# RG-LRU gates by block: features reordered, stacked remainders, tanh gates and two output phases

## The chip, the cores and the metric

One core of one Trainium2 chip runs the whole program in one launch. The metric is device time in microseconds: the median of three runs was 1885.63 us (1885.54 to 1885.96). All rows below come from one profiled execution of 1887.7 us, whose span from first to last instruction is 1885.9 us.

## The reference

Two layers of a diffusion transformer act on 256 latent tokens (x) and 256 context tokens, model width 1024. Each layer is a half-weighted SwiGLU FFN, a mixer, and a second FFN, each behind an RMS norm with shift and scale from a conditioning vector. The mixer of layer 0 is an RG-LRU of width 1280, that of layer 1 a retention. All arithmetic is float32. The part that matters here:

```python
def block_diag(x, w, b):                     # 8 blocks of 160 features
    xg = x.reshape(bsz, t, LRU_BLOCKS, LRU_BLK)
    return (jnp.einsum('btgi,gij->btgj', xg, w) + b).reshape(bsz, t, D_RNN)

def lru_coeffs(xc, gate_w, gate_b, lam):     # for each of two directions
    r = jax.nn.sigmoid(block_diag(xf, gate_w[0], gate_b[0]))
    ig = jax.nn.sigmoid(block_diag(xf, gate_w[1], gate_b[1]))
    log_a = -LRU_C * r * jax.nn.softplus(-lam)
    a = jnp.exp(log_a)
    b = jnp.sqrt(-jnp.expm1(2.0 * log_a)) * (ig * xf)
...
    # h = a*h + b forward and backward over the tokens, the context first;
    # xc is a 4-tap convolution over tokens of h @ w_x
    gate = jax.nn.gelu((h @ w_g))
    return (hsum * gate) @ w_out
```

## The kernel before

Activations lie features on partitions, tokens (256 context, then 256 latent) along the free dimension. A weight is a 128x128 tile; eight of them are one 512 KB transfer. Every product of two float32 numbers is done as three TensorE products of rounded parts (`mm3`, L140 to L144): high x high, high x low, low x high. The high part of a weight tile is a ScalarE copy (L112), the low part a VectorE subtraction (L138). `w(key)` (L117) hands out the next weight: it fetches and splits two tiles ahead (LA = 2), emits the low parts in the second half of a tile, and calls `pump` (L160), which takes one step each from two background lists, `bgv` (steps that begin on VectorE) and `bga` (ScalarE). So the order of work on each engine is the order in which the Python code emits it; engines run in order and wait for each other by semaphores. PSUM has eight banks of 512 columns, handed out in a ring.

`lru` (L534) works on ten chunks of 128 features. `first_group` computes four chunks of projections in two halves of tokens. Then, for chunk j: one projection for the Gelu gate, `gates(j)` (L596), the gates' evaluation `coeffs(j)` on ScalarE (Sigmoid four times, Exp twice, Tanh twice, Sqrt), a projection for a convolution (`conv`, L566), and the vector steps of the chunk before (L646), with the scans. A block of 160 features lies across chunks of 128, so `gates(j)` multiplies two or three row chunks for each column chunk (L37), 26 pairs in all, most of a tile being zeros. The output projection comes in three phases: chunks 0 and 1 before j = 6, chunks 2 to 5 behind the loop, and 6 to 9 in `boundary` (L404), which works in two halves of 256 tokens, sums squares for the next norm (`sq_acc`, `stat`), and begins the next FFN's inputs (`h_chunk`). `out_proj` (L359) adds each product to x on VectorE (L393).

In the two places where only the latent tokens go on (behind the retention, and at the end), `boundary` sums squares over eight chunks on VectorE, sums over partitions by a product with ones (L296), takes the inverse root on VectorE (L305 to L316), and keeps TensorE running with ten products of zeros (`warm`, L319) before `bcast` spreads the result.

## Time and profile before

| | |
|---|---|
| median of three runs | 1885.63 us |
| profiled execution | 1887.7 us, span 1885.9 us |
| TensorE busy | 1857.2 us (98%) |
| VectorE busy | 1283.8 us (68%) |
| ScalarE busy | 718.2 us (38%) |
| GpSimd busy | 0.2 us |
| mean granted TensorE clock | 0.991 of 2.4 GHz |

PE is TensorE, PEld its weight loads, DVE VectorE, ACT ScalarE. A busy share over the span is a mean over stages with different limits; the stretches tell more. A matmul's duration includes its way through the array, so the time one costs is the distance to the next one's start.

### The profile page before, as it was taken

To read this page: it belongs to the slowest core of one execution; us is meant where nothing else is said; L and a number is where in the kernel's file an instruction comes from. 1 tells how busy PE (TensorE), PEld (TensorE's weight loads), DVE (VectorE), ACT (ScalarE), POOL (GpSimd) and SP (SyncE) were. 2 spreads that over 40 slices of the span, in tenths; PEclk is the share of its full clock that TensorE was granted. 3 is DMA by queue.
4 is the path that set the end of the run, shared out by engine and by line. 5 is a ranking of instruction groups with operands and counts; after the bars stand their busy time and mean duration, and the time that the engine had idled before them with its cause. 6 is when DMAs were issued, how large, how long until landed. Compare 5 with 4: busy or idle time off the path is not lost.

```text
span 1885.9 us, 25731 instructions
## 1 busy us (share of the span) xinstructions
PE 1857.2 (98%) x10278; PEld 1621.5 (86%) x10278; DVE 1283.8 (68%) x2110; ACT 718.2 (38%) x984; POOL 0.2 (0%) x4
## 2 busy tenths in 40 slices
PE   8999999999999899999999999999999999999998
PEld 7888888897888888888889888888898899989997
DVE  7877697676899975767577655455576465675555
ACT  3322222248989342222224322222244243344442
POOL 0000000000000000000000000000000000000000
PEclk8999999999999999999999999999999999999999
DMA  8355454422322244454452445444324333355552
GB/s 319 127 211 187 167 189 181 145 90 79 100 90 90 79 157 168 158 185 172 143 172 94 154 150 187 145 171 178 102 80 150 124 123 118 97 160 182 176 186 101
DMA packets 77736, 277.52 MB, mean 147 GB/s; under 512 B 8752, under 2 KB 10032, under 8 KB 77616
## 3 DMA queue, kind: packets, MB, share of 16 engines
q1 hardware_dynamic: 77616, 275.88, 42.5%
q8 instruction: 80, 1.31, 0.3%
q14 instruction: 40, 0.33, 0.1%
HBM read 274.80 MB, written 1.05 MB: 146 GB/s over the span
## 4 chain that ended last, share of the span: by engine, by line
PE 92%; DVE 5%; ACT 1%; issue 1%; DMA 0%; SPq 0%; ACTq 0%; DVEq 0%
PE ps L142 30%; PE ps L144 30%; PE ps L143 30%; PE ps L237 1%; DVE x L393 1%; DVE wlo L138 1%; DVE hlo L138 1%; DVE h L354 0%; ACT h L348 0%; DVE acc L286 0%; PE ps L323 0%; PE ps L329 0%; PE ps L296 0%; DVE ht L346 0%; DMA x<-xt 0%
## 5 line engine op out<-in xcount | busy, mean ns | idle before, releaser
L142 PE MATMUL ps<-h,whi 128*128 128x512 f32 (+1 forms) x1824 | 641.1, 352 | 0.0
L144 PE MATMUL ps<-h,wlo 128*128 128x512 f32 (+1 forms) x1824 | 639.7, 351 | 1.2 <-DVE wlo L138 1.2
L143 PE MATMUL ps<-h,whi 128*128 128x512 f32 (+1 forms) x1824 | 640.3, 351 | 0.5 <-DVE h L354 0.5
L138 DVE TENSOR_TENSOR wlo<-wraw,whi 128x1024 fp32r<-128x1024 f32 x349 | 417.7, 1220 | 78.3 <-ACT whi L112 78.2
L112 ACT ACTIVATE whi<-wraw 128x1024 fp32r<-128x1024 f32 x349 | 357.3, 1050 | 275.8 <-PE ps L143 225.6
L144 PEld LDWEIGHTS ps<-h,wlo 128*128 128x128 f32 x1824 | 345.8, 190 | 47.7 <-DVE wlo L138 1.9
L143 PEld LDWEIGHTS ps<-h,whi 128*128 128x128 f32 x1824 | 345.9, 190 | 46.5 <-DVE h L354 1.6
L142 PEld LDWEIGHTS ps<-h,whi 128*128 128x128 f32 x1824 | 345.9, 190 | 44.9 <-ACT whi L112 0.3
L242 DVE SCALAR_TENSOR_TENSOR junk<-modraw,cB 128x1024 bf16<-128x1024 f32 x240 | 293.1, 1221 | 4.6
L393 DVE SCALAR_TENSOR_TENSOR x<-ps,M,x 128x256 f32<-128x256 f32 x296 | 132.5, 479 | 160.7 <-PE ps L144 160.3
L157 ACT ACTIVATE A<-sil 128x512 fp32r<-128x512 f32 (+1 forms) x88 | 50.9, 579 | 474.0 <-DVE sil L486 474.0
L142 PE MATMUL ps<-A,whi 128*128 128x512 f32 (+1 forms) x608 | 217.9, 358 | 0.0
L143 PE MATMUL ps<-A,whi 128*128 128x512 f32 (+1 forms) x608 | 217.9, 358 | 0.0
L144 PE MATMUL ps<-A,wlo 128*128 128x512 f32 (+1 forms) x608 | 217.9, 358 | 0.0
L486 DVE TENSOR_TENSOR sil<-ps,sil 128x512 f32<-128x512 f32 (+1 forms) x88 | 54.8, 623 | 159.8 <-PE ps L144 151.9
L144 PEld LDWEIGHTS ps<-A,wlo 128*128 128x128 f32 x608 | 114.9, 189 | 16.9
L143 PEld LDWEIGHTS ps<-A,whi 128*128 128x128 f32 x608 | 114.9, 189 | 16.9
L142 PEld LDWEIGHTS ps<-A,whi 128*128 128x128 f32 x608 | 114.9, 189 | 16.7
L158 DVE TENSOR_TENSOR A<-sil,A 128x512 fp32r<-128x512 f32 (+1 forms) x88 | 55.1, 626 | 56.7 <-ACT A L157 56.7
L485 ACT ACTIVATE sil<-ps 128x512 f32<-128x512 f32 (+1 forms) x88 | 47.3, 538 | 80.4 <-PE ps L144 79.9
L348 ACT ACTIVATE h<-ht,M 128x256 fp32r<-128x256 f32 x88 | 42.4, 504 | 91.5 <-DVE ht L346 91.5
L142 PE MATMUL ps<-A,hhi 128*128 128x256 f32 x192 | 54.8, 285 | 0.0
(171 smaller groups left out, 2065.3 us busy)
## 6 DMA issues: line engine op xcount, KB each, us to landing
wraw<-w SPq DMA_DIRECT2D x371, 512.0 KB, 4.3
modraw<-modw SPq DMA_DIRECT2D x144, 512.0 KB, 4.3
x<-xt SPq DMA_DIRECT2D x8, 256.0 KB, 4.9
mask<-mask SPq DMA_DIRECT2D x4, 512.0 KB, 6.0
out<-fin SPq DMA_DIRECT2D x8, 128.0 KB, 1.8
cs<-rope SPq DMA_DIRECT2D x1, 256.0 KB, 2.6
vecs<-vecs SPq DMA_DIRECT2D x1, 251.0 KB, 7.4
ident<-ident SPq DMA_DIRECT2D x1, 64.0 KB, 2.0
```

Source lines behind the costliest of these rows:

```text
L112: nc.scalar.activation(hi, raw, AF.Copy)
L138: self.nc.vector.tensor_tensor(lo, raw, hi.bitcast(F32), ALU.subtract)
L142: mm(ps, whi, xhi, start=first, stop=False, skip_group_check=True)
L143: mm(ps, whi, xlo, start=False, stop=False, skip_group_check=True)
L144: mm(ps, wlo, xhi, start=False, stop=last, skip_group_check=True)
L157: self.nc.scalar.activation(hi, src, AF.Copy)
L158: self.nc.vector.tensor_tensor(lo, src, hi.bitcast(F32), ALU.subtract)
L242: nc.vector.scalar_tensor_tensor(self.junk, raw, 1.0, self.cB[:, c, :], op0=ALU.mult, op1=ALU.mult, accum_out=M[:, idx, k, c:c + 1])
L348: nc.scalar.activation(h[:, 0, a:b], tt, AF.Identity, bias=M[:, 3 * n, k, c:c + 1])
L393: nc.vector.scalar_tensor_tensor(self.x[d][:, a0:a1], ps[:, a0 - c0:a1 - c0], M[:, gidx, d, c:c + 1], self.x[d][:, a0:a1], op0=ALU.mult, o ...
L485: nc.scalar.activation(s[:, :w], pa[:, c0:c1], AF.Silu)
L486: nc.vector.tensor_tensor(s[:, :w], pg[:, c0:c1], s[:, :w], ALU.mult)
```

## The change

The 1280 features are put in another order: first the leading 128 features of each block of 160 (chunks 0 to 7), then the eight remainders of 32, four to a chunk (chunks 8 and 9). A block's gate needs five column groups: four gates of 128 columns, and one group that holds the four gates' remainders of 32 columns each. The rows of the block are its 128 features, by `mm3`, and its 32 remainder features, whose three products are stacked along the contraction: `S` holds high, low and high parts of the remainder on partitions 0 to 95 (three copies by DMAs that GpSimd issues), and the weight tile holds the remainder rows three times, of which rows 64 to 95 are turned into the low part. So a block takes 5 x 3 + 5 products of 512 columns. Chunk 8's vector steps run with block 3, chunk 9's with block 7.

The sigmoids become tanh of half the argument, 1 + tanh is folded into scales and vector steps; `1 - r` moves from VectorE to ScalarE; the convolution reads its taps from PSUM without a copy to `cbuf`. Two buffers R instead of three. The output comes in two phases: chunks 0, 1, 2, 3, 8 before block 6, and the rest at the end, where chunks 4, 5, 6 are summed over all 512 tokens into eight banks (`out_sum`) and chunks 7 and 9 are added in `boundary`. Where only latent tokens go on, the last chunk's squares go to the partition sum as a second operand instead of an addition, and nine warm products follow instead of ten. There are 368 weight transfers instead of 371.

```diff
+LRU_PERM = np.concatenate([np.arange(160 * b, 160 * b + P) for b in range(8)]
+                          + [np.arange(160 * b + P, 160 * b + 160) for b in range(8)])
+LRU_ORDER = (0, 1, 2, 3, 8, 4, 5, 6, 7, 9)
...
     def w_low(self):
-            self.nc.vector.tensor_tensor(lo, raw, hi.bitcast(F32), ALU.subtract)
...
+                if kinds[o]:
+                    sub(hi[64:96, c], raw[64:96, c], hi[64:96, c].bitcast(F32), ALU.subtract)
+                else:
+                    sub(lo[:, c], raw[:, c], hi[:, c].bitcast(F32), ALU.subtract)
...
     def sq_acc(self, st, d, c0, c1):
+            if d == KD - 1 and st.get("two"):
+                st["last"] = s
+                return
...
+    def out_sum(self, acts, key):
+
+        banks = [self.psum() for _ in range(KD)]
+        for i, act in enumerate(acts):
+            for d in range(KD):
+                self.mm3(banks[d], *self.w(key(i, d)), *act(0, 2 * T), i == 0, False)
+        return banks
...
-            y = self.stat(st[0]["acc"], 2, 1.0 / D)
-            self.warm(10)
+            y = self.stat([st[0]["acc"], st[0]["last"]], 2, 1.0 / D)
+            self.warm(9)
...
-        banks = self.first_group([wx(0), wx(1), wg(0), wg(1)], False, hooks)
+        banks = self.first_group([wx(8), wx(0), wx(1), wg(0)], False, hooks)
...
             def first():
-                nc.scalar.activation(buf[:, :, 1:T + 1], p3, AF.Copy)
-                nc.scalar.activation(x, ps, AF.Identity, bias=cb[:, j:j + 1], scale=cw[:, j, 1:2])
+                act(x, ps, AF.Identity, bias=cb[:, j:j + 1], scale=cw[:, j, 1:2])
                 tap(0)
...
+        def stack_x(b):
+
+            t = S[b] = pool.tile([P, 512], F32R, tag="S", name="S", bufs=2)
+            src = xs[8 + b // 4]
+            q = slice(32 * (b % 4), 32 * (b % 4) + 32)
+            for i, part in enumerate((0, 1, 0)):
+                nc.gpsimd.dma_start(t[32 * i:32 * i + 32], src[q, part])
...
+        def gates(b):
+
+            out = [self.psum() for _ in range(5)]
+            for g in range(5):
+                self.mm3(out[g], *self.w(("lg", b, g)), xs[b][:, 0], xs[b][:, 1], True, False)
+            for g in range(5):
+                w, _ = self.w(("ls", b, g))
+                nc.tensor.matmul(out[g], w[0:96], S[b][0:96], start=False, stop=True, skip_group_check=True)
+            if b % 4 < 2:
+                stack_x(b + 2)
             return out
...
+        def gate(b, g, ps):
+
+            t = (R, I)[g % 2][b]
+            act(t[:, g // 2], ps[g], AF.Tanh, bias=gb[:, b, g:g + 1], scale=0.5)
+
+        def gate_rem(b, g, ps):
+            t = (R, I)[g % 2][8 + b // 4]
+            q = 32 * (b % 4)
+            act(t[q:q + 32, g // 2], ps[4][32 * g:32 * g + 32], AF.Tanh,
+                bias=self.gbr[32 * g:32 * g + 32, b:b + 1], scale=0.5)
...
+                act(A[c][:, d], R[c][:, d], AF.Exp, scale=sp4[:, c, d:d + 1], bias=sp4[:, c, d:d + 1])
...
+            out = [lambda a=a: gelu(*a) for a in pgs]
+            out += [with_ready(lambda: (alloc(b, R, "r", 2), gate(b, 0, ps)),
+                               lambda c: c < 2 or c - 2 in ydone, b), lambda: gate(b, 2, ps)]
...
+            out += [lambda g=g: gate_rem(b, g, ps) for g in range(4)]
+            cs = [b] + ([rem] if b % 4 == 3 else [])
+            out += [with_ready(lambda c=c: (exp(c, 0), exp(c, 1)), after(2, scandone), c) for c in cs]
+            out += [lambda c=c: (tanh(c, 0), tanh(c, 1)) for c in cs]
+            out += [lambda c=c: sqrt(c) for c in cs]
...
             sv = [
-                lambda: tt(b["i"], b["i"], xb, ALU.mult),
-                lambda: stt(b["r"], b["a"], 1.0, b["r"], op0=ALU.add, op1=ALU.mult),
-                lambda: (tt(b["s"], b["s"], b["i"], ALU.mult), ixdone.add(j)),
-                lambda: nc.vector.tensor_scalar(b["a"], b["r"], -1.0, 1.0, op0=ALU.mult, op1=ALU.add),
...
+                lambda: (stt(r, a, 1.0, r, op0=ALU.add, op1=ALU.mult),
+                         act(a, r, AF.Identity, bias=1.0, scale=-1.0)),
+                lambda: stt(i, i, 1.0, xb, op0=ALU.add, op1=ALU.mult),
+                lambda: (tt(q, q, i, ALU.mult), ixdone.add(c)),
+                lambda: stt(q, a, 1.0, q, op0=ALU.add, op1=ALU.mult),
...
+        todo = ((("x", 2), ("g", 2)), (("x", 3), ("x", 9)), (("x", 4), ("g", 3)), (("x", 5), ("g", 8)),
+                (("x", 6), ("g", 4)), (("x", 7), ("g", 5)), (("g", 6), ("g", 7)), (("g", 9),))
+        prev = []
+        for b in range(8):
+            if b == 6:
+                out([0, 1, 2, 3, 8])
+            self.bg_until(lambda: b in convdone and 8 + b // 4 in convdone)
+            g = gates(b)
+            self.bg_until(lambda: not self.bga)
+            for c in prev:
+                vector_steps(c)
+            self.bga.extend(scalar_steps(b, g, pgs))
+            prev = [b] + ([8 + b // 4] if b % 4 == 3 else [])
...
-        out([2, 3, 4, 5])
-        js = [6, 7, 8, 9]
+        js = [4, 5, 6]
+        self.bg_until(lambda: all(j in ydone for j in js))
+        banks = self.out_sum(acts(js), okey(js))
+        js = [7, 9]
         self.drain()
...
-        return self.boundary(acts(js), okey(js), 0, 5, 0, 2, hold=True)
+        return self.boundary(acts(js), okey(js), 0, 5, 0, 2, hold=True, banks=banks)
```

## Rows read from the trace of the kernel before

**Rows 1.** The page: TensorE's busy line, and the chain by engine.
```profile
PE 1857.2 (98%) x10278; PEld 1621.5 (86%) x10278; DVE 1283.8 (68%) x2110; ACT 718.2 (38%) x984; POOL 0.2 (0%) x4
PE 92%; DVE 5%; ACT 1%; issue 1%; DMA 0%; SPq 0%; ACTq 0%; DVEq 0%
```
**Rows 2.** Stretches: length, busy PE, PEld, DVE, ACT, POOL, granted clock, DMA.
```profile
514.02:530.96 16.94, 16.94 (x76) 13.94 (x75) 15.96 (x19) 16.82 (x21) 0.00 (x0) 1.00 0.31 91
...
440.19:613.08 172.89, 172.89 (x759) 142.10 (x757) 151.56 (x182) 157.78 (x196) 0.00 (x0) 1.00 0.30 96
613.08:628.16 15.08, 9.89 (x43) 8.20 (x41) 14.91 (x21) 2.82 (x5) 0.00 (x0) 0.81 0.26 71
628.16:651.92 23.76, 22.66 (x181) 22.25 (x182) 19.96 (x50) 10.05 (x20) 0.00 (x0) 0.98 0.34 111
651.92:678.35 26.43, 25.43 (x204) 24.45 (x203) 19.55 (x48) 12.61 (x22) 0.00 (x0) 1.00 0.39 140
```
**Rows 3.** TensorE's timeline: start, us, line, operation; 512 and 256 columns.
```profile
419.74 0.28 PE L143 MATMUL ps<-h,hhi 128*128 128x256 f32 x1
...
424.18 0.28 PE L144 MATMUL ps<-h,hlo 128*128 128x256 f32 x1
...
445.19 0.39 PE L143 MATMUL ps<-h,whi 128*128 128x512 f32 x1
...
448.14 0.39 PE L144 MATMUL ps<-h,wlo 128*128 128x512 f32 x1
```
**Rows 4.** ScalarE's timeline in one steady chunk (j = 4).
```profile
514.02 1.28 ACT L619 ACT_TABLE_LOAD   x1
515.31 1.27 ACT L619 ACTIVATE r<-ps,vecs 128x512 f32<-128x512 f32 x2
...
517.61 0.62 ACT L579 ACTIVATE cbuf<-ps 128x512 f32<-128x512 f32 x1
518.09 0.80 ACT L580 ACTIVATE xc<-ps,vecs 128x512 f32<-128x512 f32 x1
518.91 1.28 ACT L624 ACT_TABLE_LOAD   x1
520.21 1.34 ACT L624 ACTIVATE a<-r,sp 128x512 f32<-128x512 f32 x2
...
522.68 1.04 ACT L112 ACTIVATE whi<-wraw 128x1024 fp32r<-128x1024 f32 x1
...
525.55 1.06 ACT L634 ACTIVATE s<-r 128x1024 f32<-128x1024 f32 x1
```
**Rows 5.** VectorE's groups by form: shapes, count, busy us, mean ns, idle before.
```profile
L138 DVE TENSOR_TENSOR wlo<-wraw,whi 128x1024 fp32r<-128x1024 f32 x349 | 417.7, 1220 | 78.3 <-ACT whi L112 78.2
...
L486 DVE TENSOR_TENSOR sil<-ps,sil 128x512 f32<-128x512 f32 x66 | 45.5, 689 | 135.2 <-PE ps L144 129.3 <-ACT sil L485 5.9
...
L640 DVE TENSOR_TENSOR_SCAN r<-a,s 128x512 f32<-128x512 f32 x10 | 12.2, 1223 | 0.3
...
L647 DVE TENSOR_TENSOR i<-i,xc 128x1024 f32<-128x1024 f32 x10 | 12.2, 1219 | 0.0
...
L654 DVE TENSOR_TENSOR r<-r 128x512 f32<-128x512 f32 x10 | 6.9, 689 | 0.2
...
L650 DVE TENSOR_SCALAR a<-r 128x1024 f32<-128x1024 f32 x10 | 6.9, 688 | 0.0
```
**Rows 6.** The page's transfers: count, KB each, median us to landing.
```profile
x<-xt SPq DMA_DIRECT2D x8, 256.0 KB, 4.9
...
ident<-ident SPq DMA_DIRECT2D x1, 64.0 KB, 2.0
```
**Rows 7.** TensorE's timeline behind its wait in the old tail.
```profile
623.99 0.58 PE L144 MATMUL ps<-Y,wlo 128*128 128x256 f32 x1 [4.28 <-DVE wlo L138]
```
**Rows 8.** Timeline at the end: the last addition of squares, the warm products.
```profile
1873.78 0.43 DVE L286 TENSOR_TENSOR acc<-acc,sq 128x256 f32<-128x256 f32 x1 [0.21 <-ACT sq L285]
...
1874.73 4.00 PE L323 MATMUL ps<-warm_sb 128*128 128x512 bf16 x10
```

More of the change, by code (lines that the diff above doesn't have):

```diff
@@ L294, in stat @@
         ps = self.psum()
+        parts = s if isinstance(s, list) else [s]
         for j in range(ng):
-            nc.tensor.matmul(ps[:, j:j + 1], s[:, j * P:(j + 1) * P], self.ones, start=True, stop=True,
-                             skip_group_check=True)
+            for i, s in enumerate(parts):
+                nc.tensor.matmul(ps[:, j:j + 1], s[:, j * P:(j + 1) * P], self.ones, start=i == 0,
+                                 stop=i == len(parts) - 1, skip_group_check=True)
         if between:
@@ L668, in lru @@
-        for j in range(2):
-            for f in conv(j, banks[j]):
-                f()
-        gelu(0, banks[2])
-        gelu(1, banks[3])
-        prev = None
-        tail = []
-        def out(js):
-            while not all(j in ydone for j in js):
-                self.bgv.popleft()()
-            self.out_proj(acts(js), okey(js), 0, 5, [(0, 2 * T)])
-        def vector_steps(p):
-            nonlocal tail
-            _, sv, high, low = p
-            sv = list(sv)
-            if tail:
-                sv[1:1] = tail[:1]
-                sv[4:4] = tail[1:]
+                tt(Y[c][:, 1], r[:, 0], Y[c][:, 0].bitcast(F32), ALU.subtract)
@@ L688, in vector_steps @@
+                ydone.add(c)
+            sv[1:1], sv[4:4] = tail[:1], tail[1:]
             tail = [high, low]
             self.bgv.extend(sv)
-        for j in range(NR):
-            pgs = []
-            if j == 6:
-                out([0, 1])
-            n = j + 2 if j < 6 else j + 1
-            if j != 6 and n < NR:
-                pgs.append((n, self.proj(wg(n), 0, 2 * T)))
-            g = gates(j)
-            self.drain()
-            if prev is not None:
-                vector_steps(prev)
-            prev = coeffs(j, g, pgs)
-            self.bga.extend([lambda: None] * (3 if j else 0) + prev[0])
-            if j + 2 < NR:
-                px = self.proj(wx(j + 2), 0, 2 * T)
-                c = conv(j + 2, px)
-                rest = list(self.bgv)
-                self.bgv.clear()
-                self.bgv.extend(c[:3] + rest[:1] + c[3:4] + rest[1:2] + c[4:] + rest[2:])
@@ L710, in lru, with out @@
-        prev[1][0].ready = lambda: not self.bga
-        vector_steps(prev)
+        def out(js):
+            self.bg_until(lambda: all(j in ydone for j in js))
+            self.out_proj(acts(js), okey(js), 0, 5, [(0, 2 * T)])
+        for n, j in enumerate((8, 0, 1)):
+            self.bgv.extend(conv(j, banks[n]))
+        while self.bgv:
+            self.pump()
+        gelu(0, banks[3])
+        pgs = [(1, self.proj(wg(1), 0, 2 * T))]
+        todo = ((("x", 2), ("g", 2)), (("x", 3), ("x", 9)), (("x", 4), ("g", 3)), (("x", 5), ("g", 8)),
+                (("x", 6), ("g", 4)), (("x", 7), ("g", 5)), (("g", 6), ("g", 7)), (("g", 9),))
@@ new lines, in lru @@
+        prev = []
[9 more added lines that the diff above has]
+            prev = [b] + ([8 + b // 4] if b % 4 == 3 else [])
+            pgs = []
+            for kind, n in todo[b]:
+                if kind == "x":
+                    c = conv(n, self.proj(wx(n), 0, 2 * T))
+                    rest = list(self.bgv)
+                    self.bgv.clear()
+                    self.bgv.extend(c[:3] + rest[:1] + c[3:4] + rest[1:2] + c[4:] + rest[2:])
+                else:
+                    pgs.append((n, self.proj(wg(n), 0, 2 * T)))
```

230 lines of the change are left out of this document (128 added, 102 removed).

## The prediction

> **What bounds the kernel now.** I read the page's busy line and its chain first: TensorE is busy 98% of the span and holds 92% of the chain that ended last, nearly all of it the three products of `mm3` [rows 1]. So fewer products are worth their time only as long as nothing else sets the pace where they are taken out. The change acts on the RG-LRU stage, from the end of `first_group` (424.6 us) to the end of the next FFN's first group (678.35). I cut that stage into stretches [rows 2]. In the gate loop (440.19, first gate evaluated, to 613.08, last square root done) TensorE has no gap, but ScalarE is busy 157.8 of 172.9 us and VectorE 151.6. Over one steady chunk (514.02 to 530.96, sigmoid load to sigmoid load) it is 16.94, 15.96 and 16.82 of 16.94 us for TensorE, VectorE and ScalarE: all three are full. Behind the loop comes a tail (613.08 to 628.16) in which VectorE alone is full (14.9 of 15.1), then the output phase and the FFN's first group, 50.2 us together, with TensorE and VectorE both near full.
>
> **TensorE's part.** 512-column products follow each other at 0.227 us (13 steps from 445.19 to 448.14), 256-column ones at 0.120 (37 steps from 419.74 to 424.18) [rows 3]. Gates before: 26 tile pairs of row and column block x 4 gates x 3 products = 312. After: 8 blocks x (5 x 3 + 5) = 160. That is 152 x 0.227 = 34.5 us less. The last output phase has 192 products of 256 columns; after, 72 of 512 and 96 of 256 (16.3 + 11.5 against 23.0): 4.8 us more there, but js 4, 5, 6 run ahead of the last Y. All output work together: 336 products' worth of 512 columns before, less 0.4 us after. TensorE's need between first gate and last square root falls to about 620 x 0.227 = 141 us.
>
> **ScalarE's part.** Prices from one chunk's list [rows 4]: a table load 1.29 with the next operation 0.01 to 0.02 behind it; a gate 0.58 (two in 1.27, the overlap off); the copy to `cbuf` 0.48; weights' high part 0.95; square root 0.97. `Identity` with scale and bias from vectors takes 0.80 where the copy of the same bank takes 0.62, so a second vector operand on Exp and Tanh costs 0.09. Off over the loop: 10 sigmoid loads, and 2 loads each of Exp and Sqrt plus one of Gelu, since 8 blocks replace 10 chunks (15 x 1.29 = 19.4); 8 copies to `cbuf` (3.8) and one convolution (1.4); one Y (0.6); four weight tiles (4.1). On: 64 gate evaluations for 40, as the remainders need four of 32 partitions a block and time goes by columns (24 x 0.58 = 13.9); 40 second operands (3.6); `1 - r` at 1024 columns, priced as the weights' copy plus one operand, 8 x 1.05 = 8.4 (bounds 0.95 and 1.15). Net 157.8 - 29.3 + 25.9 = 154.4 us. That is 13 more than TensorE now needs: pace passes from TensorE to ScalarE. One regular block is 16.94 - 1.29 - 0.48 + 2.30 + 0.36 + 1.05 = 18.9 us, against 68 x 0.227 = 15.4 for TensorE.
>
> By the Trainium skill (ScalarE: Activation LUTs, What ACT_TABLE_LOAD costs) a switch of sets is 1.28 us and a drain of 1.38 on top. Here no such gap stands behind a load [rows 4], so the row is used; with the page's 2.66 the fifteen loads would give back 40 us instead of 19, ScalarE would be left with 134 and TensorE would keep the pace (rival B). I give that no chance of its own: the steady chunk is full without a drain.
>
> **VectorE's part.** 1024-column steps are 1.22 us and start every 1.14, the scan 1.22, 512-column ones 0.69, a weight tile's low part 1.22 [rows 5]. A chunk is four of the first, scans of 1.14 and (backward, in two pieces, estimated from the same row) 1.5, two 512-column steps and the low part at 0.6 to 0.7, some 9.2 us. `1 - r` (0.69) goes; the taps stay three, now from PSUM, where I price them the same (a 512-column product from PSUM and one from SBUF both run 0.69). A block takes 16.0. In block 4, chunks 3 and 8 fall together: 25.2 against ScalarE's 20.6, so `Identity` of chunk 4 waits for `r` of chunk 4, some 4.4 us. The cut low parts (`hi[64:96]`) add about 16 instructions of some 0.1.
>
> **The walk.** (r0 is the first gate evaluation of a block on ScalarE.) The first three convolutions run in series, 3.7 each (before 4.3 each, for two), then Gelu and three weight tiles: r0(0) = 441.0. The three copies into S for block 0 have 7 us from low part to need; a 64 KB transfer on SP lands in 2.0, a 256 KB one in 4.9 [rows 6], so I take 0 (one copy is 64 KB), and three of the longer in a row less the 7 us, 8, as the upper bound and nothing below, since nothing is taken away there; all other S have a block's time. The Trainium skill (DMA: Bandwidth & Descriptors, Anatomy of one DMA — SWDGE (gpsimd) path) has 2.0 us fixed for a copy issued by POOL; no run shows it yet, and it would hide too. POOL's queue is empty otherwise (0.2 us busy), and behind the copies on it stand only later copies; chunk 9's high part waits for the last reader of chunk 8's, long past by then.
>
> Each block is the 18.9, corrected: r0(1) = 459.2 (no Y yet: -0.6); r0(2) = 479.0 (a second convolution +1.4, no Gelu -1.8, a table load for Tanh +1.3: 19.8); r0(3) = 497.1 (Exp finds its table: -1.3; +0.5); r0(4) = 520.3 (chunk 8's Exp and Tanh 2.84 and square root 0.97; +0.5); r0(5) = 545.0 (chunk 8's `1 - r` and Y: 20.6; 4.1 to 4.4 of lag). The 0.5 from block 3 on is for r0(b), which needs the buffer of Y(b-2), two R buffers where there were three: Y's high part on ScalarE, its low part on VectorE, then the gate; behind it on ScalarE stand all of the block's evaluations. In block 5, gates 4.7, convolution 1.4, Exp and Tanh 2.84 behind a load 1.29, two weight tiles 1.9, load and square root 2.3: its square root ends at 559.5.
>
> Then `out([0,1,2,3,8])`, 120 products. Its third weight tile is split on ScalarE behind that square root (LA = 2), so TensorE waits there and does 72 products behind 560.6: 577.0; gates(6) end at 581.5. `vector_steps(5)` stand behind the evictions, so r0(6) = 583.5 (last eviction 577.9, `r` 1.2, `1 - r` 1.1, Gelu 1.9, Y 0.6 and 0.8). ScalarE has 9 us of work in these 24: 15 idle, where the old `out([0,1])` cost it 6. r0(7) = 602.0 (no convolution, two Gelus); the last block evaluates two chunks: gates 4.7, a load, Exp and Tanh 5.7, a weight tile or two, a load and the first square root at 617.4. From there VectorE (before: 15.1 for one chunk, with five pairs of evictions between): it waits for Y(6), whose copy stands on ScalarE behind the second square root, the last Gelu and a `1 - r`, to 5.1, the rest of chunk 7 5.3, chunk 9 10.7, two weight tiles 2.3: Y(9) is ready 23.4 later, at 640.8, where it was 628.2. TensorE is done with `out_sum` at about 632 and idles; when it idled 4.3 us there before, the granted clock over the tail was 0.81, so part of it ran at the 1.2 GHz level [rows 2, 7]; VectorE covers that here.
>
> From Y(9) to the end of the FFN's first group: TensorE saves 11.5 of its half-width products, but VectorE was busy 39.5 of those 50.2 us [rows 2] and loses only two weight tiles (2.4). With 8 evictions and sums in 8.2 us a half, mean and chunks behind them, h(0) is ready 18.4 after Y(9) (before 23.8, the fourth row's length) and the rest of VectorE's list follows at its own rate: 45 us for 50, with 39 (TensorE's 34 of products and the chain to h(0)'s first use) as the lower bound and 50 as the upper. End at 685.8 against 678.3: +7.5.
>
> The norm sums: at two places an addition on the path (0.43) goes, an extra pair of column sums comes (0.15), and one of ten warm products of 0.40 that end after VectorE has its root [rows 8]: -1.2 together (bounds -1.5, 0). Three weight tiles less to load hide under queues with space.
>
> Sum: +7.5 - 1.2 = +6. The profiled execution had 1887.7 (span 1885.9), the median of the runs is 1885.6; on the median: **1891.5 us**.
>
> **Rivals.** A, VectorE keeps up (faster): if its list of block 4 begins early enough, the lag (4.4), the waits for Y (2.5) and the two weight tiles in the tail (2.3) are gone, and the last output phase runs at TensorE's rate (39 instead of 45): 1876. For it: VectorE had 21 us of slack in the loop. Against: in the steady chunk it had one. It decides whether `Identity` in block 4 finds its input. B, TensorE stays the pace (faster): the whole 34.5 less, 1851. Against: 154 is more than 141. It would need ScalarE's block under 15.4. C, the change doesn't save the loads it means to: if Tanh behind Gelu brings a load of its own beside Exp's, 7 x 1.29 = 9 more: 1900. Between A and the forecast lies no change.
>
> **Chances.** Forecast 0.45, A 0.25, B 0.05, C 0.05, no measurable change 0.20. About 0.2% (3.8 us) is what runs of this kernel can tell from none. Faster 0.30, same 0.20, slower 0.50. The range reaches down through A and up to where S waits or the low clock in each wait would add 8 us: 1875 to 1899; the forecast's own is 1885 to 1899.
>
> **What would show it.** Right: 160 gate products; TensorE with gaps in the loop; ScalarE 95% busy there up to block 5 and idle some 15 us in the 40-tile output phase; a wait of `Identity` in block 4; the last Y near 641; 24 table loads. Wrong: a loop without gaps on TensorE (B), Y(9) before 630 (A), a load between Gelu and Tanh (C), products waiting for S.

## The result, and the profile after

The changed kernel takes 1918.89 us (median of 4 runs, 1918.17 to 1919.39) where the kernel before took 1885.71 beside it: a ratio of 1.0175, interval 1.0162 to 1.0188, some 33 us slower. The forecast was 1891.5. The profiled execution has a span of 1917.4 us, 31.5 more than before's 1885.9.

The page of the changed kernel, first TensorE's busy line and the chain by engine (the lines of [rows 1]), then the new copies among the transfers:

```profile
PE 1842.3 (96%) x10082; PEld 1599.4 (83%) x10084; DVE 1271.8 (66%) x2091; ACT 722.6 (38%) x991; POOL 12.0 (1%) x28
PE 62%; ACT 6%; DVE 5%; issue 1%; DMA 0%; ACTq 0%; DVEq 0%
...
S<-xs POOLq DMA_DIRECT2D x24, 64.0 KB, 2.0
```

TensorE executes 194 products fewer (by its weight loads, 10278 before and 10084 after). The chain's 62% can't be set beside the 92% of before: this chain is followed back only to 474.6 us, and its shares add up to 74%. In the loop itself they can be compared: from 474.6 to 644.4 us the three products of `mm3` hold 12.8% of the stretch, where in the kernel before, from 440 to 613 us, they hold 93.6%. Something else sets the pace of the loop now. The stretches of the changed kernel that answer [rows 2] (length, busy time of PE, PEld, DVE, ACT, POOL, granted clock, DMA): the whole gate loop, its part up to block 5's square root, the output phase up to block 6's first gate evaluation, the first 5 us of that phase, the tail of VectorE, and from Y(9) to about the end of the FFN's first group (712.2):

```profile
440.28:644.42 204.14, 163.68 (x637) 125.84 (x635) 135.51 (x165) 159.29 (x201) 8.00 (x17) 0.90 0.28 86
440.28:576.45 136.17, 109.43 (x420) 82.76 (x418) 96.44 (x114) 114.47 (x146) 8.00 (x17) 0.91 0.29 86
577.40:609.26 31.86, 30.65 (x123) 24.69 (x124) 20.06 (x31) 10.84 (x12) 0.00 (x0) 0.90 0.35 116
577.40:582.50 5.10, 3.89 (x8) 2.67 (x9) 4.53 (x7) 3.36 (x4) 0.00 (x0) 0.50 0.28 99
644.42:667.64 23.22, 15.24 (x55) 11.97 (x55) 21.40 (x23) 9.20 (x12) 0.00 (x0) 0.79 0.15 46
667.64:712.50 44.86, 42.11 (x302) 40.34 (x303) 35.90 (x90) 20.99 (x40) 0.00 (x0) 0.91 0.35 118
```

The loop grew from 172.9 to 204.1 us although none of the three engines has more than 2 us more to do in it. TensorE is down to 637 products in it (759 before), VectorE to 135.5 us (151.6), ScalarE stays at 159.3 (157.8). All three were at 88% or more before; now they are at 80, 66 and 78%. So no engine's work fills the loop: for most of it they wait for each other. The exception is the output phase (third line), in which TensorE is busy 30.65 of 31.86 us.

The waits of ScalarE from 440 to 645 us (engine, line, what it waited for: us, times, longest):

```profile
ACT a L721 <- DVE r L720: 21.5, 6, 7.3
...
ACT xs L617 <- issue: 2.8, 1, 2.8
ACT r L654 <- DVE Y L736: 2.6, 3, 1.3
```

Six of the eight `Identity` in that window (`1 - r`, L721) wait for `r`; with the tail it is 28.7 us in seven waits. The other two lines are a wait of a convolution's copy in block 1 and the waits of the first gate for the buffer of Y. The timelines of both engines around blocks 0 and 1 show what precedes each wait (start, us, engine, line, operation, idle before). ScalarE:

```profile
453.14 1.06 ACT L685 ACTIVATE s<-r 128x1024 f32<-128x1024 f32 x1
454.11 1.99 ACT L113 ACTIVATE whi<-wraw 128x1024 fp32r<-128x1024 f32 x2
458.71 1.06 ACT L721 ACTIVATE a<-r 128x1024 f32<-128x1024 f32 x1 [2.61 <-DVE r L720]
459.80 1.28 ACT L637 ACT_TABLE_LOAD   x1
461.09 0.60 ACT L637 ACTIVATE gl<-ps 128x512 f32<-128x512 f32 x1
461.58 1.26 ACT L654 ACTIVATE r<-ps,gbh 128x512 f32<-128x512 f32 x2
462.72 0.70 ACT L654 ACTIVATE i<-ps,gbh 128x512 f32<-128x512 f32 x1
463.29 1.08 ACT L113 ACTIVATE whi<-wraw 128x1024 fp32r<-128x1024 f32 x1
...
465.66 0.68 ACT L659 ACTIVATE i<-ps,gbr 32x512 f32<-32x512 f32 x1
466.36 0.68 ACT L659 ACTIVATE r<-ps,gbr 32x512 f32<-32x512 f32 x1
```

VectorE:

```profile
455.18 2.36 DVE L152 TENSOR_TENSOR wlo<-wraw,whi 128x1024 fp32r<-128x1024 f32 x2 [4.04 <-ACT whi L113]
457.46 1.22 DVE L720 SCALAR_TENSOR_TENSOR r<-a,r 128x1024 f32<-128x1024 f32 x1
...
466.72 0.82 DVE L150 TENSOR_TENSOR whi<-wraw,whi 32x640 fp32r<-32x640 f32 x1
...
506.99 0.82 DVE L152 TENSOR_TENSOR wlo<-wraw,whi 128x640 fp32r<-128x640 f32 x1
```

One turn, from one block to the next, reads so: ScalarE ends block 0's square root (454.1) and splits two weight tiles for block 1's gates. VectorE has stood idle 4.04 us for the first of them, makes both low parts, which were listed ahead of `r`, and then `r` (457.46). ScalarE, idle 2.61, does `1 - r`, then Gelu, then the first gate of block 1 (461.58). So the block's 21.3 us are ScalarE's work from first gate to square root (440.28 to 454.1, 13.8) and, one after the other, 7.5 of a round trip through VectorE and back. In these 7.5 ScalarE itself works 4.9 us and stands 2.6. Such a circle, in which each engine waits for the other's last step, is called a ring or a loop of waits below.

### The profile page after: what moved, and what is told of

It reads as the page before. It is cut to its first block, busy times and chain, and to the rows that moved or that the text cites. A ratio compares the mean times of both kernels' runs of the same rounds, so it can differ in the third digit from the quotient of the medians.

```text
span 1917.4 us, 25419 instructions
## 1 busy us (share of the span) xinstructions
PE 1842.3 (96%) x10082; PEld 1599.4 (83%) x10084; DVE 1271.8 (66%) x2091; ACT 722.6 (38%) x991; POOL 12.0 (1%) x28
## 3 DMA queue, kind: packets, MB, share of 16 engines
HBM read 273.23 MB, written 1.05 MB: 143 GB/s over the span
## 4 chain that ended last, share of the span: by engine, by line
PE 62%; ACT 6%; DVE 5%; issue 1%; DMA 0%; ACTq 0%; DVEq 0%
PE ps L159 21%; PE ps L158 21%; PE ps L157 21%; DVE wlo L152 1%; ACT whi L113 1%; ACT a L678 1%; ACT r L681 1%; ACT s L685 0%; ACT i L659 0%; DVE hlo L152 0%; ACT i L654 0%; DVE r L720 0%; ACT h L369 0%; DVE h L375 0%; ACT r L654 0%
## 5 line engine op out<-in xcount | busy, mean ns | idle before, releaser
L152 DVE TENSOR_TENSOR wlo<-wraw,whi 128x1024 fp32r<-128x1024 f32 (+2 forms) x350 | 411.6, 1199 | 96.5 <-ACT whi L113 96.2
L427 DVE SCALAR_TENSOR_TENSOR x<-ps,M,x 128x256 f32<-128x256 f32 x280 | 126.0, 479 | 168.3 <-PE ps L159 167.5
L157 PE MATMUL ps<-Y,whi 128*128 128x512 f32 (+1 forms) x96 | 39.5, 412 | 21.2 <-ACT gl L637 13.8
```

Of the source, the lines that this page charges most:

```text
L152: sub(lo[:, c], raw[:, c], hi[:, c].bitcast(F32), ALU.subtract)
L157: mm(ps, whi, xhi, start=first, stop=False, skip_group_check=True)
L427: nc.vector.scalar_tensor_tensor(self.x[d][:, a0:a1], ps[:, a0 - c0:a1 - c0], M[:, gidx, d, c:c + 1], self.x[d][:, a0:a1], op0=ALU.mult, o ...
```

## The experiments

All times are medians, and the ratios compare each kernel with the kernel before on the same chip. The first four vary the changed kernel in one place each. Two runs on the changed kernel leave out a part of the computation, and say so.

**1 - r on VectorE.**

```diff
-                         act(a, r, AF.Identity, bias=1.0, scale=-1.0)),
+                         nc.vector.tensor_scalar(a, r, -1.0, 1.0, op0=ALU.mult, op1=ALU.add)),
```

> The changed kernel with 1 - r back on VectorE (tensor_scalar, as before the change); ScalarE no longer waits for VectorE's r. Theory 1, round trip: between gate evaluations of two blocks ScalarE waits 28.7 us in all for r in Identity (7 places), behind which the next block's gates and Gelu stand; with the operation gone from ScalarE these waits and its 10 x 1.06 us of work go, VectorE gets 10 x 0.69: 1893 to 1902 us, and in the trace no wait of ScalarE for r and r0(5) some 15 us earlier. Theory 2, ScalarE is just overloaded by its own work: only the 10.6 us of work go, of which the output phase hides some: 1909 to 1913. Theory 3, VectorE sets the pace and Identity only shows it: VectorE gets 7 us more to do, 1919 to 1926.

1917.76 us, 1.0167 (1.0151 to 1.0182): a gain of 1 us, which is within the noise and which no theory had. The waits of ScalarE (440 to 645 us) say why:

```profile
ACT r L654 <- DVE Y L736: 14.5, 4, 4.5
ACT i L654 <- DVE s L723: 6.3, 2, 3.6
ACT L654 <- DVE Y L736: 4.7, 1, 4.7
```

The 21.5 us of waiting for `r` are gone, and so are 8.4 us of `Identity`'s own work on ScalarE in this window (8 of 1.056). In their place the waits at the gate evaluations have grown from 3.1 (2.6 and 0.5, L654) to 14.5 + 6.3 + 4.7 = 25.5: there are two R buffers, so block b's first gate needs Y(b-2) done, and Y(b-2)'s low part stands on VectorE behind `r`, `i` and `q i` of chunk b-1; there is one I buffer, so the i gates need `q i` of chunk b-1. Both lead back to the square root of b-1 just as `Identity` did. Block 3 began at 509.43 us, with `Identity` on ScalarE at 509.21.

**The vector steps listed ahead of the next block's gates.**

```diff
-                lambda: tt(r[:, 0], r[:, 0], gl[c], ALU.mult),
+                with_ready(lambda: tt(r[:, 0], r[:, 0], gl[c], ALU.mult), lambda k: k in gl, c),
...
-            g = gates(b)
             self.bg_until(lambda: not self.bga)
             for c in prev:
                 vector_steps(c)
+            g = gates(b)
```

> The changed kernel with Identity still on ScalarE, but in the loop the previous block's vector steps are listed before the next block's gate products, not behind them (the product with Gelu waits in the list for its Gelu). So r stands on VectorE ahead of the low parts of the gates' weight tiles. Theory 1, round trip by order: VectorE computes r as soon as the square root's block allows, Identity no longer waits 2.5 to 7 us a block: 1895 to 1908. Theory 2, ScalarE's own work sets the pace: within 4 us of the changed kernel's 1919. Theory 3, VectorE is full and something of its list must be late in any order: 1915 to 1930, and the waits move to the weights' low parts and so to TensorE.

1912.38 us, 1.0142 (1.0125 to 1.0159), 6 us gained, between the theories. The waits from 424 to 720 us, the changed kernel first, then this run:

```profile
ACT a L721 <- DVE r L720: 28.7, 7, 7.3
DVE wlo L152 <- ACT whi L113: 26.2, 10, 6.4
...
ACT a L721 <- DVE r L720: 31.1, 8, 10.5
DVE wlo L152 <- ACT whi L113: 9.5, 5, 3.7
```

VectorE waits less for the weights' high parts, but `Identity` waits no less for `r`. The place of `r` behind the low parts is worth 6 us; the round trip stays.

**Chunk 5's steps and Gelu ahead of the output phase.**

```diff
             if b == 6:
+                self.bg_until(lambda: not self.bga)
+                for c in prev:
+                    vector_steps(c)
+                prev = []
+                self.bga.extend([lambda a=a: gelu(*a) for a in pgs])
+                pgs = []
                 out([0, 1, 2, 3, 8])
```

> The changed kernel; in one place only, block 5's vector steps and Gelu 5 are listed before the 40 weight tiles of the first output phase instead of behind it and gates(6). In the changed kernel ScalarE has 10.8 us of work in the 31.9 us from the square root of block 5 to the first gate evaluation of block 6, and VectorE's steps of chunk 5 wait behind the evictions. Theory, the phase starves ScalarE and VectorE of listed work: the first gate evaluation of block 6 comes 6 to 11 us earlier after the square root of block 5 (32 to 21 to 26), and the kernel takes 1908 to 1913. Rival, the phase is bound by TensorE at its lower clock and by its weight tiles: the same 32 us, only the steps behind it shorter by 1 to 3: 1916 to 1919.

1920.04 us, 1.0178 (1.0163 to 1.0194): no gain, as the rival had it (1 us above its range, within the noise). With none of block 5's steps ahead of it on ScalarE, block 6's first gate comes at 608.42 in place of 609.26, and is now waiting for TensorE's gate products (L646):

```profile
608.42 1.27 ACT L654 ACTIVATE r<-ps,gbh 128x512 f32<-128x512 f32 x2 [5.52 <-PE ps L646]
```

**One evaluation for the four remainders** (three quarters of the remainders' gates are left out).

```diff
-            act(t[q:q + 32, g // 2], ps[4][32 * g:32 * g + 32], AF.Tanh,
-                bias=self.gbr[32 * g:32 * g + 32, b:b + 1], scale=0.5)
+            act(t[:, g // 2], ps[4], AF.Tanh, bias=self.gbr[:, b:b + 1], scale=0.5)
...
-            out += [lambda g=g: gate_rem(b, g, ps) for g in range(4)]
+            out += [lambda g=b % 4: gate_rem(b, g, ps)]
```

> The changed kernel with one evaluation of 128 x 512 in each block in place of the four remainder evaluations of 32 x 512: three quarters of the remainders' gates are left out (rows of one gate are written where four belong). ScalarE's work falls by 8 x (4 x 0.69 - 0.58) = 17 us. Theory 1, ScalarE's work beside its waits sets the block (work and round trip add up): 7 of 8 blocks shorten by about 2.2 us each, 1902 to 1906. Theory 2, VectorE with its two-sided waits sets the block and ScalarE's work is largely cover for waits: 1911 to 1918, the waits for r growing by what the gates save.

1902.10 us, 1.0087 (1.0072 to 1.0102): 17 us, all of the work that was taken away. The first block took 2.1 us less (459.69 - 440.54 = 19.15 for 21.3). What ScalarE does between first gate and square root is paid in full, since nothing lies beside it.

The next runs open the loops. **Ring open:** with `1 - r` on VectorE as in the first, and

```diff
-                               lambda c: c < 2 or c - 2 in ydone, b), lambda: gate(b, 2, ps)]
+                               lambda c: c < 2 or c - 2 in mdone, b), lambda: gate(b, 2, ps)]
...
+            out += [lambda g=g: gate_rem(b, g, ps) for g in range(4)]
             out.append(with_ready(lambda: (alloc(b, I, "i", 1), gate(b, 1, ps)),
                                   lambda c: c < 1 or c - 1 in ixdone, b))
             out.append(lambda: gate(b, 3, ps))
-            out += [lambda g=g: gate_rem(b, g, ps) for g in range(4)]
...
-                lambda: tt(r[:, 0], r[:, 0], gl[c], ALU.mult),
+                lambda: (tt(gl[c], r[:, 0], gl[c], ALU.mult), mdone.add(c)),
...
-                act(Y[c][:, 0], r[:, 0], AF.Copy)
+                act(Y[c][:, 0], gl[c], AF.Copy)
...
-                tt(Y[c][:, 1], r[:, 0], Y[c][:, 0].bitcast(F32), ALU.subtract)
+                tt(Y[c][:, 1], gl[c], Y[c][:, 0].bitcast(F32), ALU.subtract)
```

Y is now made from Gelu's buffer, so R is free one chunk earlier, and the i gates come later in ScalarE's list. R still has two buffers.

> The changed kernel with 1 - r on VectorE (as in the run before, which gained 1 us: its waits of ScalarE for r, 28.7 us, came back as waits of the first gate evaluation for Y's low part, 14.5 us against 2.6, and of the i gates for q times i, 6.3), and with these two loops opened as well: the product with Gelu is written into Gelu's buffer, so R's buffer is free one chunk earlier, and the remainder evaluations stand ahead of the i gates. Theory 1, ring of buffers: ScalarE's block and VectorE's block follow each other because each waits for the other's buffers; opened in one place it closes in the next, opened in all it runs at ScalarE's own work: the gate loop shortens by 15 to 25 us, 1894 to 1904. Theory 2, VectorE's own rate sets the block: 1913 to 1921, and VectorE has no idle in the loop.

1895.68 us, 1.0049 (1.0034 to 1.0064): 23 us gained, as the ring has it. The loop, here to the end of block 7's second square root:

```profile
440.81:622.93 182.12, 157.32 (x637) 125.13 (x635) 141.25 (x174) 152.66 (x193) 8.06 (x17) 0.92 0.31 96
```

The same stretch of the change as made is the first line above and the 1.03 us of that second square root, 205.17 us. So the loop is 23.1 us shorter. ScalarE's work in it is 7.7 us less (160.32 to 152.66), as `Identity` has left it; its idle time is 15.4 us less (44.85 to 29.46).

**The same with `1 - r` left on ScalarE** (this diff alone, without that of the first run):

> The changed kernel with the ring of buffers opened (product with Gelu into Gelu's buffer, remainder evaluations ahead of the i gates), and 1 - r left on ScalarE. Moving 1 - r alone gained 1 us, both together 23. Theory 1, two closed loops in parallel, each as long as the other: either alone gains nothing, here 1913 to 1919, with Identity still waiting some 25 us for r. Theory 2, the buffers are the cause and Identity's wait only a sign of it: 1895 to 1903.

1917.68 us, 1.0167 (1.0154 to 1.0181). The waits of ScalarE (440 to 645 us) are those for `r` again, and none for Y's low part:

```profile
ACT a L721 <- DVE r L720: 23.8, 7, 8.1
```

So each of the two edits gains about 1 us alone, which is within the noise, and both together gain 23: two loops side by side, of nearly the same length. What the earlier R and the later i gates are worth one by one was not tried, nor was a third buffer R.

**Remainders by one evaluation and copies,** nothing left out: the 128 x 512 result goes into a buffer, and four copies of 32 rows on POOL's queue put it in place.

```diff
-            act(t[q:q + 32, g // 2], ps[4][32 * g:32 * g + 32], AF.Tanh,
-                bias=self.gbr[32 * g:32 * g + 32, b:b + 1], scale=0.5)
+            u = self.tmp("rm")
+            act(u, ps[4], AF.Tanh, bias=self.gbr[:, b:b + 1], scale=0.5)
+            for g in range(4):
+                t = (R, I)[g % 2][8 + b // 4]
+                nc.gpsimd.dma_start(t[q:q + 32, g // 2], u[32 * g:32 * g + 32])
...
-            out += [lambda g=g: gate_rem(b, g, ps) for g in range(4)]
+            out += [lambda: gate_rem(b, 0, ps)]
```

> The changed kernel with one 128 x 512 evaluation for the four remainders of a block into one buffer, and four copies on POOL's queue that put its rows where they belong; nothing is left out. Theory 1, the evaluations' time on ScalarE was all of the 17 us that the run with one evaluation in place of four gained, and copies in another queue are free: 1901 to 1906. Theory 2, the copies are on the path in blocks 3 and 7, where chunk 8 and 9 are evaluated right behind their last remainder (2 to 8 us each): 1905 to 1916.

1900.04 us, 1.0074 (1.0059 to 1.0089): 19 us, and the copies (32 of 64 KB, landing in 2.0) cost nothing that can be seen.

**Output phase behind block 6's gates.**

```diff
-                lambda: tt(r[:, 0], r[:, 0], gl[c], ALU.mult),
+                with_ready(lambda: tt(r[:, 0], r[:, 0], gl[c], ALU.mult), lambda k: k in gl, c),
...
-            if b == 6:
-                out([0, 1, 2, 3, 8])
...
             self.bga.extend(scalar_steps(b, g, pgs))
+            if b == 6:
+                out([0, 1, 2, 3, 8])
```

> The changed kernel; in one place the order is changed: gates of block 6 and block 5's vector steps are listed ahead of the first output phase, so that its 120 products run on TensorE while ScalarE evaluates block 6. Theory, the phase costs because both other engines stand behind it: from the square root of block 5 to that of block 6 46 us fall to 25 to 32, the kernel takes 1900 to 1907. Rival, its time is TensorE's, restarted at the lower clock, and whatever is put ahead of it is paid behind it: 1915 to 1921.

1913.90 us, 1.0146 (1.0129 to 1.0163): 5 us, less than the theory's 12 and a little more than the rival's. Block 6's first gate comes 22.7 us earlier (586.54), block 7's only 5.0 (624.86), because its gates stand on TensorE behind the 120 products (the last of them starts at 622.6). The stretch between the two, columns as above:

```profile
586.54:624.86 38.32, 38.32 (x170) 31.72 (x169) 26.14 (x37) 23.69 (x30) 0.00 (x0) 1.00 0.39 123
```

**All three together** (the diffs of the ring, the copies and the output phase).

> The three changes of the other runs together (ring opened and 1 - r on VectorE, first output phase behind gates of block 6, remainders by one evaluation and copies). If the three causes are separate, their gains add: ring -15 to -25, phase -12 to -19, remainders -13 to -17: 1865 to 1880. If TensorE takes over the pace (141 us of products in the loop and its low-clock restarts), or VectorE does (about 151 us in the loop), the sum is cut: 1880 to 1895.

1894.26 us, 1.0041 (1.0026 to 1.0056), no better than the open ring alone within the noise: the gains don't add. From 565 to 605 us TensorE was busy without a gap, with the output's products ahead of block 7's gates, and ScalarE 21 of these 40:

```profile
565.00:605.00 40.00, 40.00 (x178) 33.09 (x177) 30.89 (x42) 21.17 (x26) 1.96 (x4) 1.00 0.44 138
```

**The first output phase in two parts,** on top of these three, and VectorE's `i` and `q i` ahead of `r`:

```diff
             sv = [
-                lambda: (stt(r, a, 1.0, r, op0=ALU.add, op1=ALU.mult),
-                         act(a, r, AF.Identity, bias=1.0, scale=-1.0)),
                 lambda: stt(i, i, 1.0, xb, op0=ALU.add, op1=ALU.mult),
                 lambda: (tt(q, q, i, ALU.mult), ixdone.add(c)),
+                lambda: (stt(r, a, 1.0, r, op0=ALU.add, op1=ALU.mult),
+                         nc.vector.tensor_scalar(a, r, -1.0, 1.0, op0=ALU.mult, op1=ALU.add)),
...
-            if b == 6:
-                out([0, 1, 2, 3, 8])
...
             self.bga.extend(scalar_steps(b, g, pgs))
+            if b == 5:
+                out([0, 1])
+            if b == 7:
+                out([2, 3, 8])
```

> The run with all three changes (1894), in which TensorE is full for 43 us from block 6's gates to block 7's (its 120 output products stand between them) and ScalarE is idle 24 of them, and full nowhere else. Here the output phase is cut in two: parts 0 and 1 behind block 5's gates, parts 2, 3 and 8 behind block 7's, beside the tail of VectorE; and VectorE does the i step and q times i first. Theory, TensorE's work then lies beside ScalarE's and VectorE's: 8 more evictions of 256 x 2 cost VectorE 7 us, block 7 begins 12 to 20 us earlier: 1878 to 1888. Rival, VectorE's list is the bound from block 4 to the end (tail 23 us plus evictions): 1888 to 1897.

1887.14 us, 1.0006 (0.9997 to 1.0015), level with before. Three runs asked what holds it there.

**6 us of VectorE's work taken away** (the backward scan and its addition in three chunks are left out):

```diff
-                lambda: scan(1),
-                lambda: tt(r[:, 0], r[:, 0], r[:, 1], ALU.add),
+                lambda: scandone.add(c) if c in (3, 8, 4) else scan(1),
+                lambda: None if c in (3, 8, 4) else tt(r[:, 0], r[:, 0], r[:, 1], ALU.add),
```

> The run with two output phases, without the backward scan and its addition in chunks 3, 8 and 4 (part of the computation left out): 3 x (1.42 + 0.69) = 6.3 us less on VectorE between 517 and 565 us, and nothing else. Theory 1, with the ring open VectorE's list sets the pace there (43.8 of 48 us busy): 1880.5 to 1883 (6.3 less than 1887.1, or 4). Theory 2, TensorE and its banks, or ScalarE, set it, and VectorE is only late by their waits: 1885.5 to 1888.

1881.21 us, 0.9977 (0.9967 to 0.9986): 5.9 of the 6.3 come back, so VectorE's list was on the path there.

**1 - r on ScalarE only where VectorE has two chunks in a row:**

```diff
+                         act(a, r, AF.Identity, bias=1.0, scale=-1.0) if c in (3, 8, 7, 9) else
                          nc.vector.tensor_scalar(a, r, -1.0, 1.0, op0=ALU.mult, op1=ALU.add)),
...
+            if c in (3, 8, 7, 9):
+                sv[0:3] = [sv[2], sv[0], sv[1]]
```

> The run with two output phases, with 1 - r on ScalarE for chunks 3, 8, 7 and 9 alone, where VectorE has two chunks in a row (r first there, then i and q times i while ScalarE does 1 - r). Takes 4 x 0.69 = 2.8 us off VectorE. Theory 1, VectorE's list is the path in both places: 1884 to 1885.5. Theory 2, the wait for ScalarE comes back in full: 1887 to 1891.

1883.80 us, 0.9993 (0.9984 to 1.0003): 3.3 us for the 2.8 taken off VectorE, as theory 1 had it.

**With that, the first output phase one block earlier:**

```diff
-            if b == 5:
+            if b == 4:
                 out([0, 1])
```

> As the run before it in this list, with the first part of the output (parts 0 and 1, 48 products, 16 evictions of 256 columns) behind block 4's gates in place of block 5's. TensorE was idle 11.6 of the 29 us from 517 to 546. Theory 1, VectorE's list is the path (evictions cost it 7 us wherever they stand in it): within 2 us of the run before it. Theory 2, TensorE's order is the path (block 5's gates and the projections behind them come earlier): 3 to 8 us faster, 1877 to 1883.

1879.55 us, 0.9968 (0.9957 to 0.9980): 4.3 us faster than the run before it, as theory 2 had it, so TensorE's order had been on the path there too. It is the only order of the changed kernel, with nothing left out, that is clearly faster than the kernel before, and 39 us under the change as it was made. From 517 to 565 us (chunks 3, 8 and 4) VectorE is now nearly full; that it sets the pace there was not tested in this order:

```profile
517.00:565.00 48.00, 43.57 (x180) 35.13 (x180) 46.35 (x65) 35.33 (x45) 5.77 (x11) 0.93 0.34 103
```

Two runs took one part to the kernel before. **Two products for three in its gates** (104 products, 23.6 us of TensorE; the product of the weights' high and the input's low part is left out):

```diff
-                    self.mm3(out[dg], whi, wlo, xs[i][:, 0], xs[i][:, 1], n == 0, n == len(rows) - 1)
+                    nc.tensor.matmul(out[dg], whi, xs[i][:, 0], start=n == 0, stop=False, skip_group_check=True)
+                    nc.tensor.matmul(out[dg], wlo, xs[i][:, 0], start=False, stop=n == len(rows) - 1,
+                                     skip_group_check=True)
```

> The kernel before the change with two of the three products of each gate tile pair (the weights' high part times the input's low part is left out): 104 products fewer, 104 x 0.227 = 23.6 us of TensorE's work in a loop in which ScalarE is busy 157.8 and VectorE 151.6 of 172.9 us. Theory 1, pace passes to the next engine: the loop shortens by no more than 172.9 - 157.8 = 15 us, and since the steady chunk has ScalarE at 16.82 of 16.94, by 3 to 10: 1876 to 1883. Theory 2, TensorE alone sets the pace of the loop: 1862 to 1866. Theory 3, gaps on TensorE bring the 1.2 GHz level and take back what is gained: 1883 to 1890.

1877.67 us, 0.9958 (0.9943 to 0.9973): 8 of 23.6 us, theory 1. Its loop ends at 603.98, 9.1 us sooner, with ScalarE busy 95% of it (440.2 to 605):

```profile
440.20:605.00 164.80, 155.54 (x657) 125.64 (x655) 151.98 (x183) 156.89 (x195) 0.00 (x0) 0.97 0.31 97
```

**The norm sums alone** (of the change's diff only what carries `two`, `last` and `parts`):

```diff
-            st = [{}]
+            st = [{"two": True}]
...
-            y = self.stat(st[0]["acc"], 2, 1.0 / D)
-            self.warm(10)
+            y = self.stat([st[0]["acc"], st[0]["last"]], 2, 1.0 / D)
+            self.warm(9)
```

> The kernel before the change with the change of the norm sums alone (two places: the last square goes to the column sum by a pair of products of its own, nine warm products for ten). Forecast by the steps of the prediction: an addition of 0.43 off the path, 0.15 of products on, one warm product of 0.40 off: -1.2 us together, 1884.1 to 1885.0. Rival, the warm products end behind VectorE's root only in the profile's count and nothing moves: within 0.5 us of before.

1883.29 us, 0.9987 (0.9978 to 0.9995), 2 us faster. The interval, 0.9 to 4.1 us, holds the 1.2 that were forecast.

## Why the prediction was wrong

**The direction held, the size did not.** Slower was the likeliest, but 1918.9 lies 20 us above the range. The walk shows where. Its own marks, forecast and measured:

| mark | forecast | measured | lost on this step |
|---|---|---|---|
| r0(0) | 441.0 | 440.3 | -0.7 |
| r0(3) | 497.1 | 509.2 | 12.8 |
| r0(5) | 545.0 | 562.9 | 5.8 |
| square root of block 5 | 559.5 | 576.4 | -1.0 |
| r0(6) | 583.5 | 609.3 | 8.9 |
| r0(7) | 602.0 | 629.8 | 2.0 |
| first square root of block 7 | 617.4 | 644.4 | -0.8 |
| Y(9) | 640.8 | 667.6 | -0.2 |
| end of the FFN's first group | 685.8 | 712.2 | -0.4 |

The steps lose 26.4 us in all. With the 7.5 that the walk had here, the changed kernel is 33.9 us behind at this mark; at the end of the span it is 31.5 behind, so 2.4 come back where the norm sums alone gave 2.

**The step that failed is "Each block is the 18.9".** It took ScalarE's own work as the length of a block, with 0.5 for the buffer of Y(b-2) and a wait of `Identity` in block 4 alone (4.1 to 4.4 us). The work was nearly right: 159.3 us in the loop for 154.4. The waits were not. ScalarE was to be 95% busy up to block 5 and is 84% (114.5 of 136.2): it stands 21.7 us. Of these, 13.8 are `Identity` waiting for `r`, in blocks 0, 1, 2 and 4 (7.29 in block 4); 4.1 are a convolution's copy waiting for VectorE's taps (2.8 of it in block 1), which the walk put at nothing, and the 2.8 stand in every run here; 2.8 are the buffer of Y, about what the 0.5 a block allowed. Plain blocks took 21.3, 20.7 and 20.6; the largest loss in one block is block 1's, 27.0 for 19.8.

What was left out is that two edits of the change each made ScalarE's next block depend on VectorE's steps of the last: `1 - r` moved behind `r` in ScalarE's queue, and R went from three buffers to two. In the kernel before, `1 - r` ran on VectorE, and ScalarE waited only once for VectorE's steps in the loop, 2.9 us:

```profile
ACT i L619 <- DVE s L649: 2.9, 1, 2.9
```

So no row showed a price, and the text went by sums: VectorE had 21 us of slack. Slack does not help where VectorE's steps cannot begin before ScalarE's square root and ScalarE's next block cannot begin before them. The prediction asked whether VectorE is fast enough (rival A); the question was in which order the two queues call on each other. Shown by the runs: neither loop opened alone helps (1.0167 both), both opened give 23 us, 15.4 of them idle time of ScalarE. That the second loop came with the third buffer's loss is read from the waits for Y; the buffer itself was not put back.

**The remainders** were priced at 0.58, the spacing of 128-partition evaluations. They run 0.68 with the next one 0.69 to 0.70 behind, no overlap: 32 x 0.11 = 3.5 us. And being on the ring they cost whole: 17 to 19 us for what one evaluation and free copies replace.

**The output phase** was 24 us to r0(6) and took 32.8, ScalarE idle 21 of 31.9 for the 15 forecast. Two things lie in it. `vector_steps(5)` stood behind the evictions; and TensorE waited for the third weight tile and ran its first products at the 1.2 GHz level (granted 0.50 from 577.4 to 582.5), 0.43 us apart where they are 0.23 apart later:

```profile
577.45 0.79 PE L157 MATMUL ps<-Y,whi 128*128 128x512 f32 x1 [3.50 <-ACT whi L113]
...
580.42 0.63 PE L157 MATMUL ps<-Y,whi 128*128 128x512 f32 x1
580.85 0.63 PE L158 MATMUL ps<-Y,whi 128*128 128x512 f32 x1
...
584.09 0.39 PE L157 MATMUL ps<-Y,whi 128*128 128x512 f32 x1
584.32 0.40 PE L158 MATMUL ps<-Y,whi 128*128 128x512 f32 x1
```

Listing the vector steps earlier gave nothing, since TensorE's products for block 6 came no sooner; so TensorE's own order and late start are enough to make the time. The trace gives the 8.9 us in parts, as an estimate: 84 of the phase's 120 products were still to do at 577.45 where the walk had 72 (12 x 0.227 = 2.7), the low level took some 2.3 (ten steps between starts in 4.6 us for 2.3), a low part held TensorE 1.2, and the first gate came 4.3 behind block 6's products for 2.0.

**What held.** That pace leaves TensorE: 23.6 us of products taken from the kernel before are worth 8. The tail: 23.2 us from the first square root of block 7 to Y(9) for 23.4; from there to the end of the FFN's first group 44.6 for 45. 24 table loads, and none between Gelu and Tanh (rival C). `Identity` at 1.056 us for 1.05, the second operand at 0.80 for 0.80. S never held up the loop: its copies land in 2.0 us, and the bound of 8 was not needed. The longest wait of a product with S, 3.10 us in block 4, ends at 516.79, just behind VectorE's cut low part of its weights (516.23 to 516.65); the copies of that S were issued from 481.1 to 482.8. The Trainium skill (DMA: Bandwidth & Descriptors, Anatomy of one DMA — SWDGE (gpsimd) path) gave 2.0 us for such a copy, which no row of before could show; 24 copies of 64 KB agree (median 2.0). On the drain that the Trainium skill (ScalarE: Activation LUTs, What ACT_TABLE_LOAD costs) states behind a table load, this trace stays with the one before: the load at 459.80 takes 1.28 and Gelu starts at 461.09.

Two slips of the prediction change nothing: its "336 products' worth" of output work counts half-width products as whole ones (it is 240 before and after, and 0.6 us less after, not 0.4), and rival C's 1900 lies outside the range.

**Where the gain of 34.5 us went.** In the change as made, TensorE's saved time has turned into idle time: it stands 40.5 of the loop's 204.1 us, where before it had no gap. With the ring open, the other engines are close behind, as they were before: ScalarE was busy 91% and VectorE 88% of the old loop [rows 2], and with products taken away there ScalarE was 95% busy and 8 us were all that came of it. The best order found takes 6 us off the kernel before, and in it VectorE is busy 46.35 of 48 us in the stretch shown above. How much TensorE's lower clock (0.90 over the loop, 1.00 before) costs by itself over the whole loop was not separated: it is low in stretches in which TensorE waits (0.87 in block 1, where it stands 5.1 us), and no run held it up without changing the waits too.

## What to carry to other kernels

When an edit moves a step to another engine or takes a buffer away, draw the loop it closes (who waits for whom until the same engine's next turn) and add up the durations around that loop; slack in an engine's sum does not shorten it. Two loops of the same length hide each other, so an undo that gains nothing clears no suspect until its neighbours are open too. What lies on such a loop is paid whole, as the 17 us of remainders were here, however idle the engine looks.

## What was not expected of the hardware

An evaluation of 32 partitions costs as much on ScalarE as one of 128, and more: it takes 0.68 us against 0.69, but the next starts 0.69 to 0.70 behind it (465.66 and 466.36 in the timeline above), where 128-partition ones follow at 0.57 (462.72 and 463.29). The small shape is not the reason. Two of the 32 remainder evaluations read and write from partition 0 up (block 0's and block 4's first), and both begin before the instruction ahead of them ends, by 0.14 us; none of the other 30 does, those included that read and write the same partitions further up. A pair behind the same copy of a weight tile, block 0's first and block 2's third (partitions 64 to 95):

```profile
442.55 1.09 ACT L113 ACTIVATE whi<-wraw 128x1024 fp32r<-128x1024 f32 x1
443.50 0.66 ACT L659 ACTIVATE r<-ps,gbr 32x512 f32<-32x512 f32 x1
...
493.04 1.06 ACT L113 ACTIVATE whi<-wraw 128x1024 fp32r<-128x1024 f32 x1
494.12 0.68 ACT L659 ACTIVATE r<-ps,gbr 32x512 f32<-32x512 f32 x1
```

The first starts 0.95 behind the copy's start, the second 1.08. The two that overlap are also the only ones that start at the partition at which the instruction ahead of them reads and writes; no run here tells that from a start at partition 0.

On VectorE too the 32 partitions save nothing: the low part cut to `hi[64:96]` takes 0.82 us for 32 x 640, as a 128 x 640 one does (466.72 and 506.99 above). The two pieces of a cut tile take 0.55 and 0.82 (at 488.21 and 488.79) for the 1.22 of a whole one, 0.15 more, so the forecast's 0.1 for each added piece was not far off.
